# Turned product order, transposes behind the next scores, and bound fp32 products in a two-layer hybrid trunk

## The chip, the core and the metric

One core of a Trainium2 chip runs the whole program in one launch. The metric is the device time of one execution in microseconds. The engines are named as in the profile: PE is TensorE, the matrix engine (PEld its weight loads), DVE is VectorE, ACT is ScalarE, POOL is GpSimd, and SP issues most of the DMAs.

## The reference

A trunk of two layers over 256 tokens with a model width of 2048. Layer 0 has differential attention and a gated MLP with a causal depthwise convolution (an FFN). Layer 1 has a gated DeltaNet and the same kind of FFN.

```python
x = x + diff_attention(rms_norm(x), ...)        # 8 heads, two score maps each, q and k of 128
x = x + conv_ffn(rms_norm(x), ...)              # 2048 -> 2 x 5504 -> 2048
x = x + gated_deltanet(rms_norm(x), ...)        # 16 q/k heads, 32 v heads of 128
x = x + conv_ffn(rms_norm(x), ...)

def gated_deltanet(h, ...):
    qkv, z, b_gate, a_gate = split(h @ w_in)
    qkv = silu(causal_dwconv(qkv, conv_w))      # four taps
    q, k = l2_norm(q), l2_norm(k)
    o = gated_delta_rule(q, k, v, g, beta)      # a triangular system for each head, solved in fp32
    o = rms_norm(o) * silu(z)
    return o @ w_out
```

All inputs and results are float32.

## The kernel before, in words

**Dense products.** Every large product is computed from split operands. A weight tile comes from memory as `raw`. ACT rounds it into `whi` (L104), DVE takes the rest as `wlo` (L105), and activations lie as two parts, `a[:, 0]` (high) and `a[:, 1]` (low). For each tile TensorE adds hi times high, lo times high and hi times low. `dense` (L130 to L132) goes through the weights in chunks of four tiles of 128 rows, with two output tiles: 24 products of 256 columns a chunk. Tiles of weights lie in rings of four (`RING`). `dense_tok` (L218) does the same for outputs that lie by tokens, with 512 columns and chunks of two tiles; there the activations are the stationary operand, and of its three products the first two have the same stationary part.

**Background work.** After each chunk `dense` calls `tick`, and each generator in `bg` is advanced by one step. Generators hold the work between the dense products: norms, scores, transposes, the delta rule. A step's instructions come in the program's order at the tick in which they are issued; a planner then simulates the engines and moves an instruction behind others when its inputs are late. `issue_after` and `add_manual_dep` add edges that it keeps. PSUM has two tiles of two banks for dense results (`dps`) and four banks for all else (`mp`).

**Attention.** `weigh` computes for a head two score maps (L447, L448), the two softmaxes and their difference. Two ticks later three transposes in fp32 (L467) and one copy by DVE (L468) make `aT`. `values` (L478, L479) uses `aT` after the v products.

**DeltaNet.** 16 q/k heads go in four batches of four. A batch's dense products are, in this order: k (and q) of four heads, v of the first head, z for both groups of two heads, v of the other three, and then the output products `out` of the batch before. After the fourth batch two `out` follow each other. A k head has 4 ticks, and so has a v head; z has 16 ticks for both groups, and `out` has 16 ticks in 8 blocks. The delta rule of a batch consists of these generators:

- `keys` for each head: squares, a sum over the head by TensorE (L312), decays and norms on ACT and DVE up to the product of norm and head (L604), and then four fp32 products (L611, L612), whose results DVE multiplies into `lt` and `qkt`. POOL gathers diagonal blocks into `Cc` (L622).
- `invert`: 60 dependent steps on DVE (L639, L642) invert 32x32 blocks, two transposes on DVE follow (L646, L648), and `join` puts blocks together with small products on TensorE: L677 and then L686 and L690 (32x32 tiles), then L703 and L705 (64x64 tiles), with copies by DVE and ACT between.
- `to_tokens` for each v head: four transposes (L720) and a copy to `vt`.
- `group` for two heads: the products of L740 in five steps with a copy or a subtraction between, a normalisation, a multiplication by z (L775), eight transposes (L785), and the split into `oc` (L788, L789), which `out` reads.

Between two product steps of `group` stand two `yield`s, between those of `join` one.

## Time and profile before

| | |
|---|---|
| median of three executions | 2633.92 us (2633.77 to 2635.47) |
| the profiled execution | 2633.52 us |
| its span, first to last instruction | 2631.7 us |
| TensorE's granted clock | 1.000 |
| PE busy | 2623.4 us (100%), 22318 instructions |
| DVE busy | 1839.1 us (70%) |
| ACT busy | 1451.5 us (55%) |
| POOL busy | 94.5 us (4%) |
| moved by DMA | 485.34 MB, mean 184 GB/s |

The attention takes the first 400 us of the span, the first FFN lasts until about 1095, the DeltaNet until about 1936, and the second FFN fills the rest. A line of a timeline has the start in us, the length in us (of one instruction or of a run of equal ones), engine, line, operation, names, shape and count, and in brackets the idle time before it and what ended it. TensorE's instructions overlap in their pipeline: the recorded length of one is longer than the distance to the next, so that the distance between starts is the cost of one in a row.

### The profile page before, as it was taken

To read this page: it belongs to the slowest core of one execution; us is meant where nothing else is said; L and a number is where in the kernel's file an instruction comes from. 1 tells how busy PE (TensorE), PEld (TensorE's weight loads), DVE (VectorE), ACT (ScalarE), POOL (GpSimd) and SP (SyncE) were. 2 spreads that over 40 slices of the span, in tenths; PEclk is the share of its full clock that TensorE was granted. 3 is DMA by queue.
4 is the path that set the end of the run, shared out by engine and by line. 5 is a ranking of instruction groups with operands and counts; after the bars stand their busy time and mean duration, and the time that the engine had idled before them with its cause. 6 is when DMAs were issued, how large, how long until landed. Compare 5 with 4: busy or idle time off the path is not lost.

```text
span 2631.7 us, 53562 instructions
## 1 busy us (share of the span) xinstructions
PE 2623.4 (100%) x22318; PEld 2564.5 (97%) x22318; DVE 1839.1 (70%) x2714; ACT 1451.5 (55%) x1992; POOL 94.5 (4%) x188
## 2 busy tenths in 40 slices
PE   9999999999999999999999999999999999999999
PEld 9998999999999999999989989989999999999999
DVE  7875567777777555589788787688677777776444
ACT  7665555555555444485664764674555555554333
POOL 0000000000000000011011011021000000000000
PEclk9999999999999999999999999999999999999999
DMA  7555566666666666656465465465466666666665
GB/s 247 167 171 176 157 197 194 195 195 195 193 194 194 195 196 190 192 181 192 133 188 170 143 193 161 156 184 170 147 194 193 195 196 194 193 193 200 199 203 153
DMA packets 138100, 485.34 MB, mean 184 GB/s; under 512 B 15712, under 2 KB 19584, under 8 KB 137856
## 3 DMA queue, kind: packets, MB, share of 16 engines
q1 hardware_dynamic: 137280, 481.42, 60.3%
q8 instruction: 174, 2.85, 0.4%
q14 instruction: 70, 0.57, 0.1%
q10 hardware_dynamic: 576, 0.49, 0.1%
HBM read 479.72 MB, written 2.13 MB: 183 GB/s over the span
## 4 chain that ended last, share of the span: by engine, by line
PE 99%; ACT 0%; DMA 0%; DVE 0%; issue 0%; SPq 0%; ACTq 0%
PE ps L132 28%; PE ps L131 27%; PE ps L130 27%; PE ps L218 10%; PE mp L740 2%; PE ps L175 1%; PE mp L312 1%; PE mp L612 1%; PE mp L703 0%; PE mp L705 0%; PE mp L720 0%; PE mp L611 0%; PE mp L448 0%; PE mp L478 0%; PE mp L785 0%; DMA raw<-w_first 0%
## 5 line engine op out<-in xcount | busy, mean ns | idle before, releaser
L105 DVE TENSOR_TENSOR wlo<-raw,whi 128x1024 fp32r<-128x1024 f32 (+1 forms) x903 | 1100.2, 1220 | 617.1 <-ACT whi L104 613.5
L104 ACT CAST whi<-raw 128x1024 fp32r<-128x1024 f32 (+1 forms) x903 | 943.8, 1047 | 1005.8 <-PE ps L132 847.3
L132 PE MATMUL ps<-h,whi 128*128 128x256 f32 x4224 | 1169.5, 277 | 0.0
L130 PE MATMUL ps<-h,whi 128*128 128x256 f32 x4224 | 1169.4, 277 | 0.0
L131 PE MATMUL ps<-h,wlo 128*128 128x256 f32 x4224 | 1169.0, 277 | 0.0
L131 PEld LDWEIGHTS ps<-h,wlo 128*128 128x128 f32 x4224 | 793.0, 188 | 1.5
L130 PEld LDWEIGHTS ps<-h,whi 128*128 128x128 f32 x4224 | 793.0, 188 | 1.4 <-ACT qkr L419 0.2
L132 PEld LDWEIGHTS ps<-h,whi 128*128 128x128 f32 x4224 | 793.0, 188 | 0.6
L130 PE MATMUL ps<-ac,whi 128*128 128x256 f32 x1632 | 450.3, 276 | 0.0
L131 PE MATMUL ps<-ac,wlo 128*128 128x256 f32 x1632 | 450.2, 276 | 0.0
L132 PE MATMUL ps<-ac,whi 128*128 128x256 f32 x1632 | 450.0, 276 | 0.0
L131 PEld LDWEIGHTS ps<-ac,wlo 128*128 128x128 f32 x1632 | 306.3, 188 | 0.0
L130 PEld LDWEIGHTS ps<-ac,whi 128*128 128x128 f32 x1632 | 306.3, 188 | 0.0
L132 PEld LDWEIGHTS ps<-ac,whi 128*128 128x128 f32 x1632 | 306.1, 188 | 0.0
L218 PE MATMUL ps<-whi,h 128*128 128x512 f32 x768 | 240.3, 390 | 0.0
L218 PEld LDWEIGHTS ps<-whi,h 128*128 128x128 f32 x768 | 144.0, 188 | 29.8
L218 PE MATMUL ps<-wlo,h 128*128 128x512 f32 x384 | 150.2, 391 | 0.0
L130 PE MATMUL ps<-oc,whi 128*128 128x256 f32 x512 | 143.4, 280 | 1.1 <-ACT oc L788 1.1
L132 PE MATMUL ps<-oc,whi 128*128 128x256 f32 x512 | 143.0, 280 | 0.6 <-DVE oc L789 0.6
L293 DVE SCALAR_TENSOR_TENSOR cv<-u,fcols,cv 128x255 f32<-128x255 f32 (+1 forms) x344 | 142.8, 477 | 0.0
L131 PE MATMUL ps<-oc,wlo 128*128 128x256 f32 x512 | 142.4, 278 | 0.0
L138 DVE TENSOR_TENSOR u<-ps,rstd 128x512 f32<-128x512 f32 x118 | 81.4, 690 | 38.5 <-PE ps L132 37.7
(208 smaller groups left out, 2064.7 us busy)
## 6 DMA issues: line engine op xcount, KB each, us to landing
raw<-w_up SPq DMA_DIRECT2D x344, 512.0 KB, 4.4
raw<-w_down SPq DMA_DIRECT2D x160, 512.0 KB, 3.7
raw<-w_in SPq DMA_DIRECT2D x128, 512.0 KB, 4.4
raw<-w_z SPq DMA_DIRECT2D x64, 512.0 KB, 4.1
raw<-w_out SPq DMA_DIRECT2D x64, 512.0 KB, 3.7
raw<-w_qk SPq DMA_DIRECT2D x56, 512.0 KB, 4.3
raw<-w_v SPq DMA_DIRECT2D x32, 512.0 KB, 3.7
raw<-w_o SPq DMA_DIRECT2D x32, 512.0 KB, 4.2
```

The costliest lines, as they stand in the source:

```text
L104: self.cast = nc.scalar.copy(hi, raw)
L105: self.low = nc.vector.tensor_tensor(lo, raw, hi.bitcast(F32), ALU.subtract)
L130: nc.tensor.matmul(o, hi[:, k, s], a[:, 0, :], start=first, stop=False)
L131: nc.tensor.matmul(o, lo[:, k, s], a[:, 0, :], start=False, stop=False)
L132: nc.tensor.matmul(o, hi[:, k, s], a[:, 1, :], start=False, stop=last)
L138: self.nc.vector.tensor_tensor(u, ps[:, :, :T], self.rstd.unsqueeze(1).to_broadcast([P, 2, T]), ALU.mult)
L175: nc.tensor.matmul(pss[c // 2][:, c % 2, :T], l[:, k, c * P:(c + 1) * P], acts(k0 + k)[:, i, :], start=k0 + k == 0 and l is hi and i == 0, ...
L218: nc.tensor.matmul(ps[:, c, :], l, r[:, k, :], start=first and not j, stop=last and j == 2)
L293: nc.vector.scalar_tensor_tensor(out[:, j:], u[:, :T - j], taps[n - 1 - j], out[:, j:], ALU.mult, ALU.add)
L312: last = self.nc.tensor.matmul(out, self.onesr, p[:, j], start=i + j == 0, stop=i + j == n)
L612: nc.tensor.matmul(p[:, P:384], k[:, :P], r, start=True, stop=True)
L740: nc.tensor.matmul(p[:, v, :], l(v), r[:, v, :], start=i == 0, stop=i == len(terms) - 1)
```

## The change

1. `dense` turns the order of the three products of a tile: hi times low first, then hi times high, then lo times high.
2. All products and transposes go through `mm` and `tr`, which remember TensorE's last product. While `bound` is set, each one gets an edge to the one before it, so that the planner can't move anything between; with `pin`, the first dense product after a bound run gets such an edge too.
3. In attention the three transposes and their copy become `turned`. For all heads but the last, they are issued and bound right behind the next head's second score products.
4. Generators may `yield RUN`. Such steps are resumed only at ticks that are a multiple of `period`, after all other steps of the tick. `period` is 2 in the DeltaNet, and 1 in the last batch from its first v head on. They are bound while `pin` is set: from the second batch on, and not in the last batch's v, z and `out` part. The fp32 products of `keys`, `join`, `to_tokens` and `group` are such steps. In `group` one such yield stands where two plain ones stood.
5. With `pin`, `keys` and the transposes of `group` wait one more tick and `join` seven. The copies by POOL in `join` (L670, L672) stand ahead of these seven.
6. A group of the second and third batch waits until all four v heads of its batch are in tokens, so that both groups go at the same ticks; in the first batch the second group starts after the first one's second product step. `w0` gets two buffers.
7. The scratch for DMA descriptors is halved.

```diff
+    def queue(self, ins):
+        if self.bound or self.resume:
+            self.tc.add_manual_dep(ins.ins, self.last.ins.name, ORDER)
+            self.resume = self.bound and self.pin
+        self.latest = ins
+        if self.bound or not self.aside:
+            self.last = ins
+        return ins
+
+    @contextmanager
+    def behind(self):
+        last, self.last, self.bound = self.last, self.latest, True
+        yield
+        self.last, self.bound, self.resume = last, False, False
...
     def tick(self):
-        for g in list(self.bg):
-            if next(g, self) is self:
-                self.bg.remove(g)
+        self.ticks += 1
+        self.aside = True
+        for kind in (None, RUN):
+            self.bound = self.pin and kind is RUN
+            for task in list(self.bg):
+                if task[1] is kind and task[2] < self.ticks and (kind is None or self.ticks % self.period == 0):
+                    task[1:] = [next(task[0], self), self.ticks]
+                    if task[1] is self:
+                        self.bg.remove(task)
+        self.bound = self.aside = False
...
-                nc.tensor.matmul(o, hi[:, k, s], a[:, 0, :], start=first, stop=False)
-                nc.tensor.matmul(o, lo[:, k, s], a[:, 0, :], start=False, stop=False)
-                nc.tensor.matmul(o, hi[:, k, s], a[:, 1, :], start=False, stop=last)
+                self.mm(o, hi[:, k, s], a[:, 1, :], start=first, stop=False)
+                self.mm(o, hi[:, k, s], a[:, 0, :], start=False, stop=False)
+                self.mm(o, lo[:, k, s], a[:, 0, :], start=False, stop=last)
...
+                    if s and late:
+                        with self.behind():
+                            late.pop()()
...
+                if h < nh - 1:
+                    late.append(turned)
+                    return
+                yield
+                yield
+                turned()
...
                 nc.vector.tensor_tensor(c, c, sq, ALU.mult)
                 q, k = c[:, 0, :], c[:, 1, :]
                 yield
-                yield
+                if self.pin:
+                    yield
+                yield RUN
...
                         nc.gpsimd.tensor_copy(Tas[i][quad[s], :, quad[s]], tcc[quad[s], ms[i], :])
-                yield
+                for _ in range(7 if self.pin else 0):
+                    yield
+                yield RUN
                 pp = small(32)
...
-                while mark not in joined:
+                while mark not in joined or len(ready) < (hb if 0 < mark < nb - 1 else (gi + 1) * gh) or mark == 0 and gi and steps[mark, gi - 1] < 2:
                     yield
-                yield
+                steps[mark, gi] = 0
+                yield RUN
...
-                w0 = gd.tile([P, gv, P], F32, tag="w0", name="w0", bufs=1)
+                w0 = gd.tile([P, gv, P], F32, tag="w0", name="w0", bufs=2)
...
-                yield
-                yield
+                steps[mark, gi] = 1
+                yield RUN
                 p = prod([(lambda v: sub[v][0][:, T:], w0)])
...
                 yield
-                yield
+                if self.pin:
+                    yield
+                yield RUN
                 for v0 in range(0, n, 2):
...
+                    last = b == nb - 1 and op != "k"
+                    self.period, self.pin = 1 if last else 2, b > 0 and not last
...
-                   dynamic_dma_scratch_size=2048)
+                   dynamic_dma_scratch_size=1024)
```

## The prediction

> **What bounds the kernel now.** I read the page's first part, then the busy time by stretch, the groups by line, and TensorE's timeline where dense and fp32 products meet.

> ```profile
> PE 2623.4 (100%) x22318; PEld 2564.5 (97%) x22318; DVE 1839.1 (70%) x2714; ACT 1451.5 (55%) x1992; POOL 94.5 (4%) x188
> PE 99%; ACT 0%; DMA 0%; DVE 0%; issue 0%; SPq 0%; ACTq 0%
> L132 PE MATMUL ps<-h,whi 128*128 128x256 f32 x4224 | 1169.5, 277 | 0.0
> L130 PE MATMUL ps<-h,whi 128*128 128x256 f32 x4224 | 1169.4, 277 | 0.0
> L131 PE MATMUL ps<-h,wlo 128*128 128x256 f32 x4224 | 1169.0, 277 | 0.0
> L105 DVE TENSOR_TENSOR wlo<-raw,whi 128x1024 fp32r<-128x1024 f32 (+1 forms) x903 | 1100.2, 1220 | 617.1 <-ACT whi L104 613.5
> L104 ACT CAST whi<-raw 128x1024 fp32r<-128x1024 f32 (+1 forms) x903 | 943.8, 1047 | 1005.8 <-PE ps L132 847.3
> ```

> TensorE is idle for 8.3 of 2631.7 us, and the chain of waits is TensorE for 99%. ACT's casts wait for TensorE to free a ring slot (847.3 us), so nothing upstream limits. Only TensorE's own time can move the end: its idle, the price of each change between dense and fp32 work, and its pace.

> ```profile
> 400.90:1094.00 693.10, 693.10 (x6115) 693.05 (x6114) 450.88 (x597) 352.37 (x460) 0.00 (x0) 1.00 0.66 192
> 1681.00:1696.00 15.00, 15.00 (x127) 15.00 (x127) 9.94 (x15) 8.87 (x13) 0.00 (x0) 1.00 0.64 207
> ```

> Columns: stretch, its length, busy time and count of PE, PEld, DVE, ACT, POOL, then clock. Two products are cut by each stretch's edges, so the first FFN runs 6113 products in 693.1 us, 113.4 ns each. Nothing there can be gained. Inside the delta rule there is a slower pace, 125 in 15.00 us, 120 ns each.

> **The turned order.** Chunk products now go hi·a1, hi·a0, lo·a0: same count, same operands. The three old neighbour pairs (hi to lo, lo to hi, hi to next hi) all cost 277 ns by the records. The new pair keeps the same stationary tile twice; the token products (L218) already do that for half their pairs:

> ```profile
> L218 PE MATMUL ps<-whi,h 128*128 128x512 f32 x768 | 240.3, 390 | 0.0
> L218 PE MATMUL ps<-wlo,h 128*128 128x512 f32 x384 | 150.2, 391 | 0.0
> L218 PEld LDWEIGHTS ps<-whi,h 128*128 128x128 f32 x768 | 144.0, 188 | 29.8
> ```

> No load is skipped there and both forms last the same, so I take 0. The low part of the weights is needed 113 ns later than before, but L131 never waited for it. Ends: minus 1 us, and the slow pace, which I keep as a rival. The halved DMA scratch is free: the page lists no GpSimd transfers.

> **Transposes behind the next head's scores.** Seven heads. Before, a head's three transposes made one or two separate changes into fp32. One change is priced here:

> ```profile
> 1653.49 0.28 PE L130 MATMUL ps<-oc,whi 128*128 128x256 f32 x1
> 1653.61 0.27 PE L785 MATMUL mp<-con,zt 128*128 128x128 f32 x1
> 1653.63 0.36 PE L131 MATMUL ps<-oc,wlo 128*128 128x256 f32 x1
> 1653.83 0.28 PE L132 MATMUL ps<-oc,whi 128*128 128x256 f32 x1
> 1884.74 0.82 PE L785 MATMUL mp<-con,zt 128*128 128x128 f32 x6
> L468 DVE COPY aT<-mp 128x384 f32<-128x384 f32 x8 | 4.4, 554 | 2.9 <-PE mp L467 2.9
> ```

> From 1653.49 to 1653.83 are two dense products (0.227) and one transpose: 0.34, so about 113 to 119 ns for a transpose that costs 109 in a row ((0.82-0.27)/5). A change costs about 10 ns; 14 fewer are 0.15 us. The copy behind them (0.55 us each on DVE) moves by a head; values are read long after. Ends: 0 and minus 0.3.

> **The join, batches two and three.** Its 64x64 steps:

> ```profile
> 1431.71 0.28 PE L132 MATMUL ps<-oc,whi 128*128 128x256 f32 x1
> 1431.92 1.14 PE L703 MATMUL mp<-Ta,lt 64*64 64x64 f32 x16
> 1432.99 0.38 PE L130 MATMUL ps<-oc,whi 128*128 128x256 f32 x1
> 1433.21 0.28 PE L131 MATMUL ps<-oc,wlo 128*128 128x256 f32 x1
> 1437.89 2.07 PE L705 MATMUL mp<-TT,qs 64*64 64x64 f32 x32
> 1422.26 1.13 PE mp L677 x64
> 1427.83 0.66 PE mp L690 x21
> ```

> Sixteen more L705 add 0.93 us (2.07 less 1.14), 58 ns each. L703 takes 1.50 us from dense to dense, 0.23 of it dense and 0.93 its own: 0.34 us for entering and leaving the small shape. The chain's last two rows show alternation: L690 stays in one quadrant at 31 ns each, L677 alternates two and takes 18. Bound, the middle step has to run L703 and L705 alternately, on different halves of rows and columns, so 32 should take about 1.0 us instead of 1.9. I take minus 0.95, and 0.34 for one entry fewer, in each of two batches: minus 2.6. Ends: 0 (they do not overlap, and DVE's copy comes between) and minus 2.8. [...]

> **Groups bound, both together in batches two and three.** Their tokens, five product steps and transposes now come every second tick, in one stretch for two groups (hence two w0).

> ```profile
> 1487.78 0.28 PE L131 MATMUL ps<-h,wlo 128*128 128x256 f32 x1
> 1488.45 0.30 PE L785 MATMUL mp<-con,zt 128*128 128x128 f32 x1 [0.39 <-DVE zt L775]
> 1489.07 0.27 PE L785 MATMUL mp<-con,zt 128*128 128x128 f32 x1
> 1489.66 0.49 PE L785 MATMUL mp<-con,zt 128*128 128x128 f32 x3
> 1490.22 0.49 PE L785 MATMUL mp<-con,zt 128*128 128x128 f32 x3
> ```

> Eight transposes came in four stretches; with five products, a group makes about nine, two groups 18, and now five or six. Some 24 changes fewer in two batches at 10 ns to 30 ns are 0.2 to 0.7; the slow pace, which sets in behind such changes (0.84 us in the 125 products above), may go or grow. I take minus 1.0; ends minus 2 and plus 1. The wait for zt at 1488.45 (the product before starts at 1487.78, so 0.55 us lost) has a tick more: minus 0.5.

> **The last batch,** period 1 and unbound, one tick instead of two between steps:

> ```profile
> 1886.62 0.39 PE L130 MATMUL ps<-oc,whi 128*128 128x256 f32 x1 [1.07 <-ACT oc L788]
> 1887.08 0.28 PE L131 MATMUL ps<-oc,wlo 128*128 128x256 f32 x1
> 1887.96 0.38 PE L132 MATMUL ps<-oc,whi 128*128 128x256 f32 x1 [0.60 <-DVE oc L789]
> ```

> The last six transposes start at 1884.74 and need 0.65, so 1.2 us is lost before 1886.62, and 0.77 before 1887.96. The group's last five steps are issued three ticks earlier, 3 x 24 x 113 ns = 8 us, which exceeds both: minus 2.0. Ends: minus 2.0 and 0 (if ACT and DVE are late anyway).

> **The sum.** 0 - 0.15 - 2.6 - 1.0 - 0.5 - 2.0 = -6.3 us, if the bound steps find their inputs. Against the profiled execution (2633.52; its span 2631.7 and 1.8 around it) 2627.2; that execution is 0.4 under the median 2633.92, so the forecast is 2627.6.

> **What the waits could cost.** Bound, an fp32 step stands at a fixed place, and the next chunk's first product stands behind it; behind that on TensorE's queue all of the first output tile's sums, then the ring slots, the casts on ACT and the weight loads on SP. A head's keys products now come at the sixth tick after its dense (16.3 us of products), and inputs were later:

> ```profile
> 1491.73 0.28 PE L132 MATMUL ps<-h,whi 128*128 128x256 f32 x1
> 1512.98 0.68 DVE L604 TENSOR_TENSOR cv<-cv,qs 128x512 f32<-128x512 f32 x1
> 1516.77 0.47 PE L132 MATMUL ps<-h,whi 128*128 128x256 f32 x1
> 1545.29 0.69 DVE L604 TENSOR_TENSOR cv<-cv,qs 128x512 f32<-128x512 f32 x1 [2.66 <-ACT qs L599]
> 1517.00:1529.00 12.00, 12.00 (x103) 11.84 (x102) 11.86 (x22) 10.55 (x17) 3.46 (x8) 1.00 0.59 189
> 1608.22 2.16 DVE L648 STREAM_TRANSPOSE tcc<-Ti 128x1024 f32<-128x1024 f32 x1
> ```

> Batch three's second head ends its dense at 1491.73 and has its keys at 1513.66, 21.9 us later; the fourth 1516.77 and 1545.98, 29.2 later. Six ticks with their fp32 work take about 18.5 (an estimate: some 2 us of it fp32), so 3.4 to 10.7 us are missing while DVE is full (11.86 of 12). The join's first step stands 26 ticks behind the fourth head, 71 us and some 5 of fp32, at about 1592; its input came at 1610.38, 18 late, of which 12 come back if the keys go 12 us earlier. The cover: only the chunk's first product is tied. The second output tile's 12 products (1.36 us a chunk) can go ahead for the four ring slots, 5.4 us. With it most waits are gone; without it ten heads at 3.4 to 10.7 and two joins at 6 would be 46 to 119 us. A stalled TensorE also spares DVE the casts, which shortens every such wait. I take 0, nearest to the before's rows, where the placement left no idle, and keep the upper end as a rival.

> **Rivals.** (1) *The gain is eaten*: the tail and the alternating steps come (minus 3 to 5), bound steps lose 0.2 to 0.5 us each at a dozen places: 2629 to 2635, no change. For it: DVE's full stretch; this holds too if the order was already nearly this one. (2) *Keys wait*: the cover is used up at the ten bound heads and TensorE idles on average 1.2 us each, 12 us: 2640; it decides from 0.65 us a head, where the 6.3 is spent. For it: the 10.7 us at the fourth head against a cover of 5.4. Against: the ring, and the keys' chain gets ACT and DVE as soon as TensorE stops. [...] (3) *The slow pace stays on in an FFN*: it sets in behind an fp32 stretch and lasted all 125 products there. An FFN's up products (43 x 96 = 4128) at 6.7 ns more are 27 us: 2655. Against: both FFNs leave it now.

> **How the numbers follow.** Forecast 0.50 (own range 2623 to 2629), rival one 0.28, two 0.15, three 0.04, the rest for a larger gain. A measurement of this kernel tells 0.2%, 5.3 us, from no change: faster is under 2628.7, slower over 2639.2. So faster 0.50, same 0.31, slower 0.19. The range for 8 in 10 goes from 2622 (all lower ends, minus 9 with margin) to 2641 (rival two's price).

> **What would show it.** After: FFN stretches at 113.4 ns still; L703 and L705's lines as one run of 32 in about 1.2 us in batches two and three; no idle before the first product on oc of the last out; fewer, longer fp32 runs. Wrong if: TensorE shows idle ended by DVE's L604 or L648 lines in the k and v stretches, or 120 ns products over hundreds, or a clock under 1.00.

## The result, and the profile after

| | before | after |
|---|---|---|
| median of four executions each | 2634.22 us (2633.77 to 2635.47) | 2661.38 us (2659.85 to 2663.71) |
| ratio, with its 95% interval | | 1.0099 (1.0087 to 1.0111) |
| span of the profiled execution | 2631.7 us | 2661.9 us |
| PE busy / idle in it | 2623.4 / 8.3 us | 2633.7 / 28.2 us |
| granted clock | 1.000 | 0.995 |

The change costs 27 us, 1%. In the profiled executions the span grows by 30.2 us: 19.9 us are idle time of TensorE, 10.3 us are more busy time. TensorE was busy for some 25 us at half the clock (in the stretches shown below, and for 3.4 us from 11.2 us on, before any bound step), which costs about 12.5 us (an estimate: half of that time); the rest is time gained elsewhere. In the changed kernel all products stand at L76 and all transposes at L79, the helpers that record them. L604 has become L652, L105 and L104 are L141 and L140, L648 is L698, L789 is L840. The rows that answer to those of the first part:

```profile
PE 2633.7 (99%) x22318; PEld 2570.8 (97%) x22318; DVE 1843.8 (69%) x2714; ACT 1448.8 (54%) x1988; POOL 96.5 (4%) x188
PE 95%; ACT 2%; DVE 2%; issue 1%; DMA 0%; SPq 0%; ACTq 0%; DVEq 0%
```

The chain that ended last had 99% TensorE; now 4% of it are DVE and ACT, so TensorE waits for them at places where it did not. The view of waits (line that waited, what it waited for, us in total, times, the longest) says where:

```profile
PE mp L76 <- DVE cv L652: 9.6, 5, 4.0
PE ps L76 <- DVE wlo L141: 5.3, 7, 1.0
PE ps L76 <- ACT whi L140: 2.9, 4, 1.8
PE mp L76 <- DVE Ta L745: 2.1, 1, 2.1
PE ps L76 <- DVE oc L840: 2.1, 1, 2.1
```

The first row is the keys' products waiting for L652, the line that the prediction named as the sign of rival two. The second is dense products whose cast came late. The fourth is the join of batch one, which ends among batch two's k heads and is bound there. Of these the kernel before had 1.5 us for whi at its start, and 1.1 and 0.6 us of the last row (at L788 and L789).

The timeline at the end of batch one's join and at the fourth head of batch two, then busy time by stretch (stretch, length, busy time and count of PE, PEld, DVE, ACT, POOL, granted clock, DMA share, GB/s):

```profile
1255.99 0.70 PE L76 MATMUL mp<-Ta,lt 64*64 64x64 f32 x9 [2.13 <-DVE Ta L745]
...
1340.97 0.63 PE L76 MATMUL mp<-qp,onesr 128*128 128x512 f32 x2
1347.55 0.68 DVE L652 TENSOR_TENSOR cv<-cv,qs 128x512 f32<-128x512 f32 x1
1348.38 2.10 PE L76 MATMUL mp<-cv 128*128 128x128 f32 x8 [4.05 <-DVE cv L652]
```

```profile
400.90:1094.00 693.10, 693.10 (x6115) 693.05 (x6115) 451.99 (x597) 353.08 (x460) 0.00 (x0) 1.00 0.65 192
1252.00:1257.00 5.00, 2.87 (x114) 2.79 (x111) 4.14 (x7) 3.06 (x6) 1.01 (x2) 1.00 0.50 152
1257.00:1270.70 13.70, 13.03 (x85) 12.10 (x84) 3.44 (x5) 1.97 (x4) 0.00 (x0) 0.50 0.11 37
1344.30:1348.40 4.10, 0.05 (x2) 0.05 (x1) 2.68 (x4) 3.41 (x8) 0.00 (x0) 1.00 0.67 186
1349.20:1352.70 3.50, 3.50 (x11) 2.84 (x10) 3.50 (x10) 1.91 (x2) 1.41 (x5) 0.51 0.35 131
1560.90:1567.70 6.80, 5.13 (x14) 4.32 (x15) 6.80 (x16) 2.90 (x5) 2.14 (x7) 0.50 0.44 146
```

The FFN is the same to the hundredth. From 1344.30 to 1348.40 TensorE does nothing, and behind that wait it runs at 0.51 for 3.5 us. Behind the 2.13 us at 1256 it runs at half for 13.7 us. Batch three's fourth head repeats the first picture at 1562.57, with 6.8 us of half clock. Going by the position of each head's last dense product in the two traces, batch two's four k heads, in which batch one's join and groups end, cost 10.6 us more than before, its first v head and z 5.8, batch three from its third k head to z 11.5, and batch four there 2.7. In between, from a batch's third v head to the next batch's second k head, 2.1 and 2.0 us were gained.

### The profile page after: what moved, and what is told of

It is laid out like the page before. It is cut to its first block, busy times and chain, and to the rows that moved or that the text cites. A ratio compares the mean times of both kernels' runs of the same rounds, so it can differ in the third digit from the quotient of the medians.

```text
span 2661.9 us, 53566 instructions
## 1 busy us (share of the span) xinstructions
PE 2633.7 (99%) x22318; PEld 2570.8 (97%) x22318; DVE 1843.8 (69%) x2714; ACT 1448.8 (54%) x1988; POOL 96.5 (4%) x188
## 3 DMA queue, kind: packets, MB, share of 16 engines
HBM read 479.72 MB, written 2.13 MB: 181 GB/s over the span
## 4 chain that ended last, share of the span: by engine, by line
PE 95%; ACT 2%; DVE 2%; issue 1%; DMA 0%; SPq 0%; ACTq 0%; DVEq 0%
PE ps L76 90%; PE mp L76 5%; DVE wlo L141 1%; PE mp L79 1%; ACT whi L140 1%; ACT L316 0%; DVE cv L329 0%; DMA raw<-w_first 0%; ACT d L651 0%; ACT qs L646 0%; ACT d L650 0%; DMA gb<-decays 0%; DVE cv L652 0%; DMA decays<-grow 0%; ACT cv L325 0%
## 5 line engine op out<-in xcount | busy, mean ns | idle before, releaser
L141 DVE TENSOR_TENSOR wlo<-raw,whi 128x1024 fp32r<-128x1024 f32 (+1 forms) x903 | 1101.4, 1221 | 615.5 <-ACT whi L140 613.5
L140 ACT CAST whi<-raw 128x1024 fp32r<-128x1024 f32 (+1 forms) x903 | 944.1, 1047 | 1042.2 <-PE ps L76 961.1
L76 PE MATMUL ps<-h,whi 128*128 128x256 f32 (+1 forms) x8608 | 1472.1, 277 | 3.9 <-ACT whi L140 2.6
L76 PEld LDWEIGHTS ps<-h,whi 128*128 128x128 f32 (+1 forms) x8608 | 1295.9, 188 | 7.5 <-ACT whi L140 3.2
L76 PE MATMUL ps<-h,wlo 128*128 128x256 f32 x4288 | 1177.0, 277 | 3.3 <-DVE wlo L141 3.3
L76 PEld LDWEIGHTS ps<-h,wlo 128*128 128x128 f32 x4288 | 801.2, 188 | 5.2 <-DVE wlo L141 4.1
L76 PE MATMUL ps<-ac,whi 128*128 128x256 f32 x3264 | 555.6, 276 | 0.0
L76 PEld LDWEIGHTS ps<-ac,whi 128*128 128x128 f32 x3264 | 491.6, 188 | 0.1
L76 PE MATMUL ps<-ac,wlo 128*128 128x256 f32 x1632 | 450.2, 276 | 0.0
L76 PEld LDWEIGHTS ps<-ac,wlo 128*128 128x128 f32 x1632 | 306.3, 188 | 0.0
L76 PE MATMUL ps<-whi,h 128*128 128x512 f32 x768 | 243.5, 393 | 0.3 <-ACT whi L140 0.3
L76 PE MATMUL ps<-oc,whi 128*128 128x256 f32 x1024 | 179.2, 279 | 2.1 <-DVE oc L840 2.1
L76 PEld LDWEIGHTS ps<-whi,h 128*128 128x128 f32 x768 | 145.4, 190 | 31.3 <-ACT whi L140 1.1
L76 PEld LDWEIGHTS ps<-oc,whi 128*128 128x128 f32 x1024 | 155.0, 188 | 2.6 <-DVE oc L840 2.3
L76 PE MATMUL ps<-wlo,h 128*128 128x512 f32 x384 | 150.6, 392 | 2.0 <-DVE wlo L141 2.0
L76 PE MATMUL ps<-oc,wlo 128*128 128x256 f32 x512 | 142.3, 278 | 0.0
L76 PEld LDWEIGHTS ps<-oc,wlo 128*128 128x128 f32 x512 | 96.2, 188 | 0.1
L327 ACT ACTIVATE cv<-u,fcols 128x256 f32<-128x256 f32 x172 | 93.8, 592 | 0.4 <-DVE u L174 0.4
L329 DVE SCALAR_TENSOR_TENSOR cv<-u,cols,cv 128x254 f32<-128x254 f32 (+2 forms) x192 | 84.8, 489 | 11.5 <-ACT cv L325 11.4
L76 PEld LDWEIGHTS ps<-wlo,h 128*128 128x128 f32 x384 | 72.8, 190 | 17.5 <-DVE wlo L141 2.9
```

Of the source, the lines that this page charges most:

```text
L76: return self.queue(self.nc.tensor.matmul(*args, **kwargs))
L140: self.cast = nc.scalar.copy(hi, raw)
L141: self.low = nc.vector.tensor_tensor(lo, raw, hi.bitcast(F32), ALU.subtract)
L327: nc.scalar.activation(out, u, AF.Identity, bias=bias, scale=taps[n - 1])
L329: nc.vector.scalar_tensor_tensor(out[:, j:], u[:, :T - j], taps[n - 1 - j], out[:, j:], ALU.mult, ALU.add)
```

## The experiments

Theory one: bound steps stand where their inputs are late; TensorE waits there, and its clock then falls. Theory two: the period of two ticks and the added ticks cost, not the edges. Theory three: the turned order costs. Each median below stands beside that of the kernel before on the same chip (2634.2 to 2635.6 us in all).

**Nothing bound, and the turned order alone.**

```diff
-            self.bound = self.pin and kind is RUN
+            self.bound = False
```

> The changed kernel with nothing of the delta rule bound; its steps, the period of two ticks and the added ticks stay. Theory one (bound steps stand where their inputs are late, TensorE waits there, and its clock then runs at half): the stalls at the keys, the join and the groups and the half clock go; TensorE idle 8 to 12 us instead of 28.2, clock 1.000, time 2630 (2626 to 2634). Theory two (the period of two ticks and the added ticks cost, not the edges): most of the 27 us stays, over 2650. Theory three (the turned order of a chunk's products costs): over 2650 too, but with PE busy still 10 us above before.

2635.43 us, ratio 1.0001 (0.9992 to 1.0011). Clock 1.000, and the view of waits is back at:

```profile
PE ps L76 <- DVE oc L840: 2.1, 1, 2.1
PE mp L76 <- DVE eps L55: 1.1, 1, 1.1
PE mp L76 <- DVE cv L652: 0.9, 2, 0.5
```

And in the kernel before:

```diff
-                nc.tensor.matmul(o, hi[:, k, s], a[:, 0, :], start=first, stop=False)
-                nc.tensor.matmul(o, lo[:, k, s], a[:, 0, :], start=False, stop=False)
-                nc.tensor.matmul(o, hi[:, k, s], a[:, 1, :], start=False, stop=last)
+                nc.tensor.matmul(o, hi[:, k, s], a[:, 1, :], start=first, stop=False)
+                nc.tensor.matmul(o, hi[:, k, s], a[:, 0, :], start=False, stop=False)
+                nc.tensor.matmul(o, lo[:, k, s], a[:, 0, :], start=False, stop=last)
```

> The kernel before with the turned order of a chunk's three products alone. Theories one and two: 2634 (2632 to 2636), FFN products at 113.4 ns. Theory three: 2645 or more, with idle time ahead of hi times low or products over 113.4 ns in the FFNs.

2635.27 us, ratio 1.0003 (0.9994 to 1.0013). Theories two and three fall: the loss comes from the edges. That nothing is gained without them (2630 was expected) is told below.

**Which bound step?** First the keys are freed (a third kind, resumed at the same ticks and not bound):

```diff
-        for kind in (None, RUN):
+        for kind in (None, FREE, RUN):
...
-                yield RUN
+                yield FREE
                 prods = []
```

> The changed kernel with the keys' products not bound, at the same ticks; all else bound as it is. Theory one: the two waits of 4 us for the fourth heads' L652 (1348 and 1562) and the half clock behind them (3.4 and 6.8 us) go, with part of the smaller waits ahead of late wlo behind keys: 13 to 20 us less than after, 2642 to 2648; the stalls at 1256 and 1265 and their half clock of 13.7 us stay. Theory two: 2658 to 2663.

2671.61 us, ratio 1.0139 (1.0123 to 1.0154): 10 us slower than after, where 13 to 20 less were expected. Its waits, and the timelines at the fourth head's keys and at the join's first step in batch two:

```profile
PE mp L76 <- DVE tcc L698: 13.2, 2, 6.7
PE mp L76 <- DVE cv L652: 8.7, 5, 3.8
```

```profile
1352.08 2.47 PE L76 MATMUL mp<-cv 128*128 128x128 f32 x7 [3.81 <-DVE cv L652]
...
1409.25 1.94 DVE L698 STREAM_TRANSPOSE tcc<-Ti 128x1024 f32<-128x1024 f32 x1
1411.34 1.92 PE L76 MATMUL mp<-tcc,lt 32*32 32x32 f32 x64 [6.74 <-DVE tcc L698]
```

The late wlo and their 5.3 us are gone, so they came with bound keys. But the free keys of the fourth heads still wait, 3.8 us in batch two and 1.7 in batch three where it was 4.05 and 4.04, and `join` now waits for the end of `invert`, 6.7 and 6.5 us in the two batches. The kernel after had no wait there. So the lateness wasn't the keys' own: the next bound step has it too.

The second cut binds only from batch two's z on:

```diff
-            self.bound = self.pin and kind is RUN
+            self.bound = self.pin and self.tight and kind is RUN
...
+                    self.tight = b > 1 or b == 1 and (op == "z" or op == "v" and i > 0)
```

> The changed kernel, bound only from batch two's z on: what is left of batch one's join and groups, and batch two's keys, can be moved by the planner again. Theory one: the stalls at 1147 to 1265 and 13.7 us of half clock go, and with batch two's keys free its 4.2 us at 1348 and 3.4 us of half clock; batch three's stay: 16 to 20 us less than after, 2642 to 2646. Theory two: 2658 to 2663.

2656.19 us, ratio 1.0080 (1.0064 to 1.0097). The stalls from 1256 to 1265 went with their half clock, but the fourth head's keys in batch two, which come after z has begun and so were bound, waited 5.9 us where 4.05 stood, with 10.2 us of half clock around it; batch three is as in after. It is about 5 us less than after where 16 to 20 were expected: the stalls of batch one went, those at batch two's keys stayed and grew.

**Where would the join be in time?** The keys free, and the join four ticks later:

```diff
-                for _ in range(7 if self.pin else 0):
+                for _ in range(11 if self.pin else 0):
```

> The third experiment's kernel (keys not bound) with the join's first step four ticks (10.9 us) later. Theory one, mended (all bound steps hang on one chain of DVE; with the keys free its end, tcc, is 6.7 us late for the join, and a later join is not): both waits of 6.7 us and the half clock behind them (6.8 us each) go: about 20 us less than the third experiment, 2652 (2648 to 2656); the stalls of batch one stay. Rival (the wait moves on to the groups' steps): 2660 to 2672.

2654.09 us, ratio 1.0071 (1.0057 to 1.0085): as expected 17.5 us less than the third experiment, both waits for tcc gone. With that, and bound only from batch two's z on as in the fourth, and period one in the first batch:

```diff
-                    self.period, self.pin = 1 if last else 2, b > 0 and not last
+                    self.period, self.pin = 1 if last or not b else 2, b > 0 and not last
```

> Bound are only the joins and groups of batches two and three; keys free, join four ticks later, period of one in the first batch. Theory one, mended: no wait over 1 us but the last batch's 2.2; clock 1.000; 2632 (2629 to 2636): the 2.4 us that binding gave in the products from batch two's third v head on, and 0.8 for the first batch's period, less than the kernel with nothing bound. Rival (the wait moves on to the groups, or the keys are late whatever the join does): over 2640.

2644.68 us, ratio 1.0035 (1.0023 to 1.0048), a miss: free keys still waited 4.7 us at 1342 and 1.7 at 1552, and the token transposes of batch two's second v head, still bound, 1.8 us for their cv. I took it that bound tokens, those of the first v head above all, drag the keys ahead, and freed them (in `to_tokens`):

```diff
-                yield RUN
+                yield FREE
                 p = mp()
                 for t in range(2):
```

> The seventh experiment's kernel with the token transposes free too: bound are only joins and groups of batches two and three. Theory one, third form (a bound step pulls earlier free ones ahead, since all share the four mp banks in the program's order: the bound tokens of the first v head drag the fourth head's keys to a place where cv is late): the waits of 4.8 us at 1342, 2.0 us at 1403 and 1.9 us at 1552 go, and the half clock at 1341: 11 to 13 us less than the seventh, 2632 (2630 to 2636). Rival (the keys wait for another reason): only the 2.0 us for the tokens' own cv go, 2642.

2652.86 us, ratio 1.0066 (1.0053 to 1.0079). The named waits did go, so the bound tokens had caused them (whether through the banks, as the expectation has it, is not shown). But the time is 8 us over the seventh's, where 12 less were expected: the next bound step took the lateness again, though it stands four ticks later than in after:

```profile
PE mp L76 <- DVE tcc L698: 13.8, 2, 7.4
PE ps L76 <- DVE oc L840: 2.1, 1, 2.1
```

Freeing the groups as well (`yield FREE` at all five places of `group`) changes nothing in that:

> The ninth experiment's kernel with the groups free too: bound are only the joins of batches two and three. By the prediction's sum the join brings 1.3 us a batch and the groups 0.5: the products from a batch's third v head to the next batch's second k head, which took 109.9 us with nothing bound and 108.7 with all bound (without the waits there), take 109.0 here. If the groups bring it instead: 109.7. Time 2631 to 2636.

2652.07 us, ratio 1.0064 (1.0050 to 1.0077). The time missed by the two waits for tcc (6.9 and 6.4 us). `out` and the next two k heads take 61.38, 12.65 and 11.12 us, the ninth's numbers to 0.01: binding the groups brings 0. The stretch that the expectation names took 118.0 and 118.8 us; without what the waits cost (7.04 and 6.52 us between starts) and half of the 4.79 and 7.49 us busy at clock 0.50 behind them it is 108.6 and 108.5, against 109.9 and 109.8 with nothing bound, so that by this estimate the 1.3 us a batch are the join's.

**The edge behind a bound run.** Only this one is dropped; the edges among the bound products stay:

```diff
-            self.resume = self.bound and self.pin
+            self.resume = False
```

> The changed kernel without the edge from a bound run to the next dense product; all other edges stay. If that edge is what keeps the second output tile's products from covering a late step (the cover that the prediction counted on), dense products go ahead of late steps: no wait over 1 us for L652 or Ta L745, clock 1.00, 2635 to 2642. If the order is fixed at planning time by times that do not know of the lateness, the edge does not matter: 2655 to 2662.

2634.86 us, ratio 0.9997 (0.9988 to 1.0006). Waits, and batch three's fourth head:

```profile
PE ps L76 <- DVE oc L840: 2.1, 1, 2.1
PE ps L76 <- ACT whi L140: 1.5, 1, 1.5
PE mp L76 <- DVE eps L55: 1.0, 1, 1.0
PE mp L76 <- DVE cv L652: 1.0, 1, 1.0
```

```profile
1536.88 0.39 PE L76 MATMUL mp<-qp,onesr 128*128 128x512 f32 x1
1542.74 0.68 DVE L652 TENSOR_TENSOR cv<-cv,qs 128x512 f32<-128x512 f32 x1
1548.03 1.47 PE L76 MATMUL mp<-cv 128*128 128x128 f32 x8
```

Here the cover works: 11.2 us of products lie between the head's sum and its keys, and cv is ready 4.6 us ahead. In after the same head had the sum at 1555.16 and the keys at 1562.57, 7.4 us apart, 4.04 of them idle. The opposite cut has this edge and no other:

```diff
-            self.bound = self.pin and kind is RUN
...
+        if self.pin and self.latest is not seen:
+            self.last, self.resume = self.latest, True
```

> The changed kernel with no edges among the fp32 products; only the edge from a RUN tick's last product to the next dense product stays (the opposite of the tenth experiment). If that edge alone is the price: 2661 (2657 to 2665), waits for L652 of 4 us, half clock at the same places. Rival (both kinds of edges are needed): 2635 to 2645.

2662.42 us, ratio 1.0104 (1.0090 to 1.0117), and after's waits for L652, wlo and Ta to the digit (the lines lie two further down):

```profile
PE mp L76 <- DVE cv L654: 9.6, 5, 4.0
PE ps L76 <- DVE wlo L143: 5.3, 7, 1.0
PE mp L76 <- DVE Ta L747: 2.1, 1, 2.1
```

```profile
1349.21 2.12 PE L76 MATMUL mp<-cv 128*128 128x128 f32 x8 [4.04 <-DVE cv L654]
```

So this edge alone is the price: without it nothing is lost, with it alone all of the loss is there.

**A place behind the lateness.** The eleventh's kernel, the join four ticks later once more:

```diff
-                for _ in range(11 if self.pin else 0):
+                for _ in range(15 if self.pin else 0):
```

> The eleventh experiment's kernel (bound are only the joins of batches two and three) with the join four ticks later once more, 15 plain ticks instead of 11. Theory one, last form (the edge that ties the next dense product makes TensorE bear all that a bound step's input is late at its place; a place behind the lateness costs nothing): the waits of 7.0 and 6.5 us for tcc and their half clock go, about 19 us less, and the join's 1.3 us a batch stay: 2632.5 (2630 to 2636). Rival (the lateness follows the join, since DVE's work is ordered by it): 2645 or more.

2635.61 us, ratio 1.0001 (0.9992 to 1.0010): 16.5 us less than the eleventh, no wait for tcc in its rows.

```profile
PE ps L76 <- DVE oc L840: 2.1, 1, 2.1
PE mp L76 <- DVE cv L652: 1.3, 3, 0.9
```

The tie is kept and costs nothing at a place where the input is there. The 1.3 us a batch did not show in the time, though. From the second v head's end to the next batch's first v head's end there are 26.5 us with fp32 in them against 27.2 with nothing bound, but dense products lose 2.9 us to the slow pace against 1.8 (batch two; sums of what consecutive starts exceed 113.3 ns per 256 columns).

**What halves the clock.** Ten made waits in each FFN, in the first experiment's kernel:

```diff
+        self.mm(p[:, :P], g[:, :P], self.ones, start=True, stop=True)
+        for _ in range(k):
+            self.nc.gpsimd.memset(g, 1.0)
+        self.mm(p[:, :P], g[:, :P], self.ones, start=True, stop=True)
```

> The kernel of the first experiment (nothing bound) with ten made waits in each FFN, TensorE's order held around them: a product, then 2, 3, 4, 5, 6, 7, 8, 10, 12, 16 fillings of 128x512 on POOL (0.5 us each), then a product that needs them; in the second FFN 64 products of 32x32 stand ahead of each. Theory one in the form that the earlier stalls give it (2.1 us after small products halved the clock, 2.2 us in the tail did not): waits up to 1.6 us leave the clock at 1.00, from 2.6 us on it falls for 3.4 or 6.8 us, in the second FFN somewhat earlier. [...] Rival (the clock falls for another reason than waiting, such as the changes of shape): no half clock at the first FFN's waits.

One execution took 2832.08 us: the made waits come to 87.4 us, and the granted clock is 0.972. The two rows of the timeline end waits of 2.45 and 3.03 us; the stretches are 3.41 us long, laid on the starts of the half-clock stretches:

```profile
532.54 0.80 PE L76 MATMUL mp<-ones,gap 128*128 128x128 f32 x2 [2.45 <-POOL gap L107]
581.31 0.49 PE L76 MATMUL mp<-ones,gap 128*128 128x128 f32 x2 [3.03 <-POOL gap L107]
```

```profile
528.93:532.34 3.41, 1.16 (x11) 0.96 (x9) 2.61 (x4) 2.04 (x3) 1.96 (x4) 1.00 0.54 195
532.34:535.76 3.42, 3.22 (x15) 3.22 (x16) 2.18 (x6) 0.82 (x2) 0.15 (x1) 0.50 0.46 157
576.72:580.13 3.41, 1.56 (x14) 1.37 (x13) 2.62 (x3) 2.04 (x3) 1.58 (x3) 1.00 0.64 217
580.13:583.54 3.41, 2.23 (x19) 2.23 (x20) 2.39 (x7) 0.83 (x2) 1.05 (x2) 1.00 0.54 172
583.54:586.95 3.41, 3.41 (x32) 3.41 (x32) 1.42 (x2) 1.05 (x1) 0.00 (x0) 1.00 0.02 6
2092.24:2095.65 3.41, 3.41 (x113) 3.41 (x111) 3.13 (x6) 1.73 (x3) 0.00 (x0) 1.00 0.60 191
2095.65:2099.06 3.41, 1.54 (x20) 1.19 (x16) 1.01 (x3) 0.82 (x2) 1.57 (x3) 0.50 0.38 133
```

The wait of 2.45 us lies with 2.25 us in one stretch, and the next is at half. The longer one of 3.03 us is split into 1.85 and 1.18, and nothing happens. Waits of 1.22 and 1.87 us did nothing, and from 3.61 us on each cost 6.8 or 10.2 us of half clock. The last two rows: a stretch full of 32x32 products, without idle time, is followed by half clock just so. In that FFN, the second, even the wait of 1.28 us behind 64 such products did it. So waiting does halve the clock, against the rival; but no limit on the length of a wait fits, that expected between 1.6 and 2.6 us included, since 2.45 us did it and 3.03 us did not.

The same by filling the waits: 28 products of ones ahead of the two keys' steps that wait 4 us.

```diff
                     p = mp()
+                    for _ in range(28 if self.pin and hq % hb == hb - 1 and r is k else 0):
+                        self.mm(p[:, :P], self.ones, self.ones, start=True, stop=True)
```

> The changed kernel with 28 products of ones (128 columns, 3.1 us) bound ahead of the keys' products of the fourth heads of batches two and three, which waited 4.2 us each. Theory one (the half clock is a price of its own, caused by the wait): both waits are mostly filled, the half clock at 1349 and 1561 is gone, the data come when they came: 4 to 5 us less than after, 2657 (2655 to 2659). Rival (the clock is no price, or the waits do not cause it): 2661 or more, up to 2667 if the products add to the waits.

2663.09 us, ratio 1.0107 (1.0093 to 1.0122), with the half clock gone at both places. The expectation missed since a product of ones takes 0.22 us, not 0.11 (two records each), so 28 took 6.2 us and outlasted the waits by 2.0 us each. Batch two's and three's first half of z took 0.4 us more and 0.5 less than after, so that the half clock there had cost 1.6 and 2.5 us. And at the tail, behind the last transposes of the twelfth's kernel:

```diff
                     acts += [oc[:, i] for i in range(2)]
+                if mark == nb - 1 and gr[-1] == hb - 1:
+                    with self.behind():
+                        self.warm(8)
```

> The twelfth's kernel with 8 products of ones (0.22 us each) bound behind the last eight transposes, where TensorE idles 2.1 us in every run since the change. If 2.06 us of idle inside one window of the clock gate is what halves the clock there in some executions (3.4 us at half, 1.7 us), that never happens here: 0 to 1.2 us less in the median, and no half clock in the profile at the tail. Rival: no half clock there was due to the idle, or the products delay the output products: 0.5 to 1.8 us more.

2634.14 us, ratio 0.9996 (0.9987 to 1.0005), 1.5 us less than the twelfth's median and the lowest of all, but not to be told from before. The expectation's windows are the stretches of 3.41 us seen with the made waits. The profile has no half clock at the tail, but the twelfth's has none there either; what speaks for the expectation is that ten of the eleven executions have a mean granted clock of 1.000 against four of the twelfth's eleven, whose other seven are at 0.999 and 1.6 us longer (2636.0 against 2634.4 us in the median). The tail is not the only such place: the kernel before, without this wait, has 1.000 in ten of 21.

## Why the prediction was wrong

It put the kernel at 2627.6 us in a range up to 2641; 2661.4 came. By its own steps:

- **Turned order, 0.** Right: ratio 1.0003 alone, and the first FFN's 6115 products in 693.10 us after as before.
- **Transposes behind the next scores, minus 0.15.** Not to be resolved: the start of the span alone differs by some 2 us between kernels that begin alike (1100.0 to 1102.3 us up to the first k head; after had 3.4 us of half clock in it). The reading beside the turned order, that the token products keep the same stationary tile for half their pairs, should be one pair in three; the 0 does not change by it.
- **The join, minus 2.6.** The alternation is right. Bound, L703 and L705 (both L76 here) alternate, 32 in 0.94 us by the starts where 1.0 was put:

```profile
1421.40 1.14 PE L76 MATMUL mp<-Ta,lt 64*64 64x64 f32 x16
1428.12 0.27 PE L76 MATMUL mp<-Ta,lt 64*64 64x64 f32 x1
1428.13 0.27 PE L76 MATMUL mp<-TT,qs 64*64 64x64 f32 x1
...
1429.06 0.22 PE L76 MATMUL mp<-TT,qs 64*64 64x64 f32 x1
```

  From the third v head to the next second k head, where no wait falls in after, it takes 108.66 us in both batches, against 109.94 and 109.80 with nothing bound: the 1.3 us a batch that were put. But with the tie dropped (tenth) it takes 109.59 and 109.44, and with the join at 15 ticks (twelfth) 109.38, though the products alternate in both. So the alternation alone does not bring the 1.3 us; what brings the rest is open.
- **Groups bound, minus 1.0.** 0 by the ninth against the eleventh; inside its ends.
- **The wait for zt, minus 0.5.** Right: gone in after, and with nothing bound too, so binding is not what it took.
- **The tail, minus 2.0.** Failed: the idle time is 2.07 us, against 1.07 and 0.60. Rows of after:

```profile
1889.94 0.49 PE L79 MATMUL mp<-con,cv 128*128 128x128 f32 x3
1890.59 0.27 PE L79 MATMUL mp<-con,cv 128*128 128x128 f32 x1
1901.62 1.05 PE L76 MATMUL mp<-vt,TT 128*128 128x128 f32 x8
1914.55 1.03 PE L79 MATMUL mp<-con,zt 128*128 128x128 f32 x8
1917.65 0.50 PE L76 MATMUL ps<-oc,whi 128*128 128x256 f32 x2 [2.07 <-DVE oc L840]
```

  I counted three ticks saved among the group's own steps. The second group waits for the last v head's tokens (the first two rows). They came 46.0 us after that head's last dense product (1843.98), against 33.7 before (1847.70 after 1813.97), the group's first products stand right behind them, and its third product step, at 1901.62, came 2.7 us later by the same measure instead of 8 earlier.
- **"I take 0" for the waits.** This is the step that failed, and with it the forecast. Six ticks and late inputs were right; how late was put too high (10.7 us at the fourth heads, where 4.05 were waited, and 3.4 at a second head, where 0.57 at most was). The cover was wrong. The prediction let the second output tile's products run ahead while the first tile's was tied. Next to none did: between the bound runs of batches two and three stand whole chunks of dense products, 24, 48 or more. The exceptions are two products of the next chunk that stand ahead of the first head's keys in batch three (at 1520.01 and 1520.12, 0.23 us; two more in batch four), and two whole chunks of z in each of batches two and three (24 products, from 1329.71 and from 1543.68 on), which went ahead of the third head's keys and of 48 products of v. Ahead of the fourth heads' keys, where TensorE waited 4 us, no product from behind the tie went. That the tie is what holds them back is shown by the tenth and fourteenth experiments; why the planner, which moved two such products elsewhere, moved none there was not tried, and stays open.
- **Rival two** had place, line and sign right and the size too small: 12 us, where idle time grew by 19.9 us and busy time, by the half clock, by 10.3. It counted waits at the keys. The join and groups of batch one (2.13 and 0.7 us) and dense products behind late wlo (5.3) were not in it. The half clock had no price in the forecast: behind the fourth heads' waits of 4.05 and 4.04 us it came for 3.41 and 6.83 us, and behind that of 2.13 us for 13.65.
- **Rival three**, the slow pace in an FFN, did not happen.

Not foreseen: with the tie dropped and no such wait left the kernel is not faster either. Of the join's gain 0.35 us a batch is left then, the tail's did not come, and the first batch (its four k heads and first v head) lost 0.8 to 1.4 us: 61.26 us before, 62.03 with nothing bound, 62.64 after. The period of two is not the cause, since the turned order alone took 62.17 and the kernels with a period of one there 62.2 to 63.3; the cause is open.

## What to carry to other kernels

The edge behind a late step cost everything here, and the edge ahead of it nothing: the step itself may wait for free as long as other work may pass. Before tying an order by hand, compare for each tied step the time at which its input ended with the time of its place; where the input is later, the whole engine waits, and taking the tie off one step hands the lateness to the next one on the same chain (keys, then join). A fixed place cost nothing once it lay behind the lateness (the twelfth experiment), where choosing which steps to tie left 10 to 37 us of loss.
